# One decoder layer on one core: low-part products last in ten weight tiles, bank copies ahead of casts, eight block sums on another engine, one more pair by seven products

## The chip, the cores and the metric

The kernel runs on one core of one Trainium2 chip. A core has a matrix engine (TensorE, called PE in the profile; its weight loads are called PEld), a vector engine (VectorE, DVE), an engine for activation functions and copies (ScalarE, ACT), GpSimd (POOL) and a sync engine (SP) that only starts transfers. They run side by side and meet at semaphores. The metric is the device time of one execution in microseconds; the median of several runs is given. Operands lie in SBUF (128 partitions); matmul results are gathered in the banks of PSUM, which PE, DVE and ACT reach.

## The reference

One layer over x of 512 tokens by 1024 channels, all float32:

- u = RMSNorm(x); one input projection makes the gated-linear-unit halves, q, k, v, the output gate r, a rank-16 decay and two merge gates.
- Branch A: GLU, a causal depthwise convolution of 31 taps, LayerNorm over channels, swish, a projection.
- Branch B: gated linear attention of 4 heads in chunks of 64 tokens; per head an RMS norm over its 256 value channels, times silu(r), a projection.
- Merge: sigmoid(gA) * yA + sigmoid(gB) * yB, then the projection w_o, and the residual is added.
- Channel mixer: RMSNorm, an up projection to 2 x 2816 channels, a causal convolution of 3 taps, silu(a) * b, the down projection, residual; then a last RMSNorm.

## The kernel before, in words

**Products in three parts.** To keep float32 accuracy with a faster number type, each operand is split in a high and a low part (`hi`, `lo`), and one product is three matmuls, low x high, high x low, high x high (`mm3`, L395 to L397). A column tile of weights is 128 partitions by 1024 (eight k blocks of 128), so `col_tile` issues 24 matmuls of 512 columns into one PSUM bank, k after k.

**How weights come.** The list `order` names every weight block in the order of use. `load` starts the transfer of a block into one of four `raw` buffers (SP queue). `split_weight` then makes the parts: ACT casts `raw` to `whi` (L323, L342), and DVE subtracts, `wlo` = raw - whi (L324, L351). For the tiles named in the set `ADDED` the low part is made without DVE: ACT writes -whi into `wlo` (L344), and a DMA issued by POOL adds the block from HBM onto it (L345, accumulate). Four `whi` and four `wlo` buffers turn round. `weight(name, j)` takes the next block and calls `prefetch`, which splits up to two blocks ahead.

**Seven products for eight.** Where a matrix product can be cut in 2 x 2 quarters, the kernel uses seven quarter products in place of eight (`seven` for w_o and w_down, `Inner` for w_r and w_v, `up_seven` for the column tiles i of the up projection that stand in `UP_SEVEN`). They need sums of quarters of the weights. In `seven` a run has steps a11, a12, s1, n2, s4, n3, a22, in two halves d; the operand of n2 is a block `kept` plus the block `raw` that lands for it (L277), once in each half of the four runs, eight sums in all. Blocks that are summed by transfer are added by POOL's DMAs (L270, L303). In `up_seven` DVE and POOL form the sums (L285), the partial results are copied between banks by ACT (L1566, L1569, L1572, L1576) and DVE (L1578, L1579), and between its steps `beside` issues pieces of the ordinary tile of the same pair (`by_parts`).

**The heads.** In the loop over heads, head h's queries and keys are projected while the scores, states and outputs of head h - 1 are formed. `outputs` squares each half on ACT with a running sum (L1142), DVE adds epsilon (L1144), POOL raises to -1/2 (L443), and DVE scales (L1150); `gated` turns the result with PE (L1156). `decays` runs a scan on DVE and three exponentials on ACT (L1067, L1068, L1072). The convolution's taps (DVE, L813) are handed out between weight blocks by `fill`.

**After w_o.** `o_at` is called behind the products of a step; it turns the normalised residual rows of token tile 0 (behind n3's first half tile) and of tile 1 (behind a22's first) into channel order, with PE transposes (L474), a DVE multiply by the gain (L483), an ACT cast (L485) and a DVE subtraction (L486). The up projection's first tiles read them.

**What sets the order.** The start of the kernel, and the last products, are ordered by hand (`manual_schedule`). Elsewhere a planner places each engine's instructions ahead of time, by its own estimates of when each can start; on the chip each engine then runs its list strictly in that order. `tc.issue_after(x)` puts the instructions of a block behind x on x's engine.

Of the kernel before, what the change touches and what calls it, by code (L numbers as in the profile page):

```python
# [10 lines left out]
F32 = mybir.dt.float32  # L11
# [6 lines left out]
P = 128  # L18
# [24 lines left out]
ET = mybir.EngineType  # L43
ADDED = {("w_glu", 2 * k) for k in (2, 3, 4, 6, 7)} | {("w_qk", m) for m in range(0, KT)}
ADDED |= {(name, m) for name in ("w_gb", "w_gla") for m in range(KT)}
UP_SEVEN = (6, 7, 10, 11, 14, 15, 18)
UP_BESIDE = (1, 3, 4, 5, 9, 20, 13, 16, 17)
ADDED |= {("w_up", j) for i in UP_BESIDE for j in (i, FT + i)}
SEVEN = {"w_o": KT // 2, "w_down": FT // 2, "w_r": KT // 2, "w_v": KT // 2}


# [27 lines left out]
def trunk_layer(ctx: ExitStack, tc: tile.TileContext, a: dict, out: bass.AP):  # L79
# [65 lines left out]
    gate_up = cp.tile([P, HEADS * DK], F32R, name="gate_up")  # L145
    ones = cp.tile([P, P], F32, name="ones")
    mhalf = cp.tile([P, NT], F32, name="mhalf")
    shares = cp.tile([P, P], F32, name="shares")
    run64 = cp.tile([P, T], BF16, name="run64")
    keep = cp.tile([P, P], U8, name="keep")  # L150
# [2 lines left out]
    def load_consts():  # L153
        tc.keep_in_program_order(nc.sync.dma_start(pp, a["pp"]))
        nc.gpsimd.memset(shares, -1.0 / D)
        nc.gpsimd.memset(run64, 1.0)
        nc.gpsimd.memset(run64[:, 0:T:64], 0.0)

        kf = tmp(P)
        nc.gpsimd.memset(kf, 1.0)  # L160
        nc.gpsimd.affine_select(
            kf, kf, pattern=[[1, P]], compare_op=ALU.is_ge, fill=0.0, base=0, channel_multiplier=-1
        )
        nc.gpsimd.tensor_copy(keep, kf)
        nc.gpsimd.memset(att, 0.0)
# [106 lines left out]
    def operand(name, raw, pairs, step, d):  # L272

        if step == "s4":
            return kept[name, pairs, d, "b22"]
        if step == "n2" and name not in INNER:
            nc.vector.tensor_tensor(kept[name, pairs, d], kept[name, pairs, d], raw, ALU.add)  # L277
        return raw if step in ("a12", "n3") else kept[name, pairs, d]

    def up_operand(raw, i, s):  # L280
# [24 lines left out]
    def split_weight(between=None):  # L305
        if len(ready) < len(order):
            while len(raws) <= len(ready):
                load()
            raw = raws[len(ready)]
            name, spec = order[len(ready)]  # L310
            if name in SEVEN or name == "w_up7":
                raw = operand(name, raw, *spec) if name in SEVEN else up_operand(raw, *spec)
                n = raw.shape[-1]
                if name == "w_up7" and spec[1] == "m":
                    both = wp.tile([P, D], F32R, tag="raw", name=nm("wm"), bufs=4)
                    nc.scalar.copy(both[:, :T], raw)
# [6 lines left out]
                nc.scalar.copy(hi, raw)  # L323
                pace[0] = nc.vector.tensor_tensor(lo, raw, hi.bitcast(F32), ALU.subtract)  # L324
                if name in SEVEN:
                    sum_on(name, *spec)
                skipped = name in INNER and raws[len(ready)] is None
                ready.append((hi, lo))
                if not skipped:
                    load()  # L330
                return
            hi = wp.tile([P, D], F32R, tag="whi", name=nm("whi"), bufs=4)
            if order[len(ready)][0] == "w_low":
                nc.scalar.copy(hi, raw)
                if order[len(ready)][1] == 0:
                    part_lo = lambda t: t.rearrange("p (k c) -> p k c", c=P)[:, :, :RANK]
                    nc.vector.tensor_tensor(part_lo(hi), part_lo(raw), part_lo(hi.bitcast(F32)), ALU.subtract)
                ready.append((hi, None))
                load()
                return  # L340
            lo = wp.tile([P, D], F32R, tag="wlo", name=nm("wlo"), bufs=4)
            nc.scalar.copy(hi, raw)  # L342
            if order[len(ready)] in ADDED:
                pace[0] = nc.scalar.activation(lo, raw, AF.Copy, scale=-1.0)  # L344
                nc.gpsimd.dma_start(lo, a[name][spec], accum_op=ALU.add)  # L345
                ready.append((hi, lo))
                load()
                return
# [42 lines left out]
    def mm3(acc, l, r, first, last, more=False):  # L391
# [4 lines left out]
        nc.tensor.matmul(acc, lh, rl, start=False, stop=False, **kw)  # L396
        nc.tensor.matmul(acc, lh, rh, start=False, stop=last, **kw)  # L397

    def col_tile(w, acts, acc=None, lo=0, hi=T):

        if acc is None:
            acc = mm_bank()
        for k in range(KT):
            s = slice(k * P, (k + 1) * P)
            ah, al = acts[k]
            mm3(acc[:, lo:hi], (w[0][:, s], w[1][:, s]), (ah[:, lo:hi], al[:, lo:hi]), k == 0, k == KT - 1)
        return acc

    def row_half(name, j0, n, acts, nk, done, tok_inner, middle=None):
# [641 lines left out]
    class Head:  # L1051
# [77 lines left out]
        def outputs(self):  # L1129
            self.o = tp.tile([P, NT, DV], F32, tag="x", name=nm("o"), bufs=3)  # L1130
            for g in range(2):
# [7 lines left out]
                        nc.tensor.matmul(half, flat(self.q, p, 0), self.s[p], start=False, stop=True)  # L1139
                for i in range(2):  # L1140
                    half = po[:, i * DV : (i + 1) * DV]
                    nc.scalar.activation(junk(DV), half, AF.Square, scale=1.0 / 16.0, accum_out=ss[:, i : i + 1])  # L1142
                v = small(2, "var2")
                nc.vector.tensor_scalar(v, ss, EPS, None, ALU.add)  # L1144
                r = rsqrt(v, 2)
                for i in range(2):
                    t = 2 * g + i
# [25 lines left out]
    def between(h, i):  # L1173
# [4 lines left out]
        else:  # L1178
            gate_b(6 + i)

    heads = [Head(h) for h in range(HEADS)]
    for h in range(HEADS + 1):
        old = heads[h - 1] if h else None
        new = heads[h] if h < HEADS else None
        if new:
            new.decays()
            if h == 0:
                for y in sr.values():
                    behind(lambda: nc.scalar.activation(y, y, AF.Silu))
# [167 lines left out]
    def o_at(step, i):  # L1357
        if (step, i) == ("n3", 0):
            u2.extend(new_acts())
            first = tp.tile([P, D], F32, tag="gain", name=nm("f2"), bufs=1)  # L1360
            to_channels(normed[0], u2, 0, lambda g: first[:, g * T : (g + 1) * T])
        if (step, i) == ("a22", 0):
            to_channels(normed[1], u2, 1, lambda g: btmp())

    seven("w_o", O_PAIRS, mixed, o_complete, o_at)
# [186 lines left out]
    def up_seven(i, beside, done):  # L1552
# [15 lines left out]
        ys = att.rearrange("p a c -> p (a c)")[:, :H]  # L1568
        nc.scalar.copy(ys, y)  # L1569
        step("n2", x, wx, 1, False, 1)  # L1570
        prefetch(1)
        nc.scalar.activation(n1[:, :H], x, AF.Copy, scale=-1.0)  # L1572
        step("a12", n0[:, :H], wb, 1, False, 2)
        prefetch(2)
        step("n3", x, wn, 0, False, 1)
# [10 lines left out]
    def by_parts(w):  # L1586

        acc = mm_bank()
        for k in range(KT):
            s = slice(k * P, (k + 1) * P)  # L1590
            mm3(acc, (w[0][:, s], w[1][:, s]), acts2[k], k == 0, k == KT - 1)
            yield acc

    for gi, pairs in enumerate(GROUPS):
        acts = []
# [123 lines left out]
```

## Time and profile before

| | |
|---|---|
| median of 3 runs | 831.07 us (829.67 to 834.61) |
| the profiled execution | 828.47 us |
| its span on the core | 826.8 us |
| granted TensorE clock | 0.998 |
| PE busy | 813.3 us, 4090 matmuls |
| DVE busy | 676.8 us, 991 instructions |
| ACT busy | 471.0 us, 669 instructions |
| POOL busy | 123.1 us, 144 instructions |
| read from HBM | 133.84 MB |

The span is the time from the first to the last instruction of the core; 1.7 us of the profiled execution lie around it. The busy time of PE counts overlapped matmuls once, so a PE that waits shows as a gap between starts: matmuls of 512 columns follow each other every 0.23 us, those of 256 columns every 0.12 us.

### The profile page before, as it was taken

What the parts mean: (1) busy time and instruction counts of PE and PEld (TensorE: products, weight loads), DVE (VectorE), ACT (ScalarE), POOL (GpSimd) and SP (SyncE); (2) the same over time, 40 slices, a digit from 0 to 9 for tenths busy, and PEclk for the clock granted to TensorE, in tenths of its full rate; (3) what the DMA queues carried; (4) which work ended last, traced back from release to release, by engine and by line L of the source; (5) the groups of instructions that cost most, each with busy time, mean ns of one, the idle gap of its engine ahead of it and who ended that gap; (6) DMA issues with size and microseconds to landing.
All of it is one profiled execution on the core that took longest, in us unless ns stands there. A gap on an engine that the chain in (4) does not pass through costs nothing.

```text
span 826.8 us, 11023 instructions
## 1 busy us (share of the span) xinstructions
PE 813.3 (98%) x4090; PEld 689.9 (83%) x4090; DVE 676.8 (82%) x991; ACT 471.0 (57%) x669; POOL 123.1 (15%) x144
## 2 busy tenths in 40 slices
PE   8999999999999999999999999999999999999996
PEld 7988878878888888888888898888788888988885
DVE  6898978999989889854689768789858888588896
ACT  7664546695443553359344659655446543667554
POOL 2021101311122121000001012111112111220111
PEclk9999999999999999999999999999999999999999
DMA  9999849558666578221447539356835647557562
GB/s 324 310 327 222 209 116 230 129 160 211 150 131 154 134 195 202 77 102 51 153 92 205 183 116 237 93 146 153 217 93 149 166 89 217 153 153 202 131 128 101
DMA packets 50213, 136.65 MB, mean 165 GB/s; under 512 B 4624, under 2 KB 17184, under 8 KB 50160
## 3 DMA queue, kind: packets, MB, share of 16 engines
q1 hardware_dynamic: 37456, 90.91, 31.2%
q0 software_dynamic: 12528, 44.83, 30.5%
q8 instruction: 32, 0.52, 0.3%
q10 hardware_dynamic: 176, 0.20, 0.1%
q14 instruction: 21, 0.17, 0.1%
HBM read 133.84 MB, written 6.29 MB: 169 GB/s over the span
## 4 chain that ended last, share of the span: by engine, by line
PE 78%; DVE 11%; DMA 4%; issue 3%; ACT 2%; POOL 1%; SPq 0%; POOLq 0%; ACTq 0%; DVEq 0%
PE mm L396 22%; PE mm L395 22%; PE mm L397 22%; DVE c L813 4%; PE ax L395 2%; DMA wlo<-in_w_glu_dram 2%; PE mm L663 2%; PE ax L396 2%; PE ax L397 2%; DVE wlo L324 1%; DMA kept<-rows 1%; DMA x<-in_x_dram 1%; PE ax L1137 1%; DVE tmp L1378 1%; PE ax L474 0%
## 5 line engine op out<-in xcount | busy, mean ns | idle before, releaser
L395 PE MATMUL mm<-uh,wlo 128*128 128x512 f32 (+1 forms) x636 | 237.5, 374 | 3.5 <-DMA wlo<-in_w_glu_dram 1.9
L396 PE MATMUL mm<-ul,whi 128*128 128x512 f32 (+1 forms) x636 | 234.9, 369 | 0.2 <-DVE ul L486 0.2
L397 PE MATMUL mm<-uh,whi 128*128 128x512 f32 (+1 forms) x636 | 234.5, 369 | 0.0
L813 DVE SCALAR_TENSOR_TENSOR c<-h,pp,c 128x507 f32<-128x507 f32 (+20 forms) x240 | 169.9, 733 | 2.8
L395 PEld LDWEIGHTS mm<-uh,wlo 128*128 128x128 f32 x636 | 119.9, 189 | 22.9 <-DMA wlo<-in_w_glu_dram 2.1
L397 PEld LDWEIGHTS mm<-uh,whi 128*128 128x128 f32 x636 | 119.8, 188 | 20.5
L396 PEld LDWEIGHTS mm<-ul,whi 128*128 128x128 f32 x636 | 120.1, 189 | 18.7 <-DVE ul L486 0.7
L342 ACT CAST whi<-raw 128x1024 fp32r<-128x1024 f32 x94 | 97.4, 1042 | 36.7 <-PE mm L397 29.0
L344 ACT ACTIVATE wlo<-raw 128x1024 fp32r<-128x1024 f32 x47 | 49.5, 1058 | 69.6 <-PE mm L395 65.5
L323 ACT CAST whi<-raw 128x1024 fp32r<-128x1024 f32 (+1 forms) x53 | 54.0, 1027 | 52.6 <-PE mm L397 36.1
L324 DVE TENSOR_TENSOR wlo<-raw,whi 128x1024 fp32r<-128x1024 f32 (+1 forms) x53 | 65.8, 1249 | 11.5 <-ACT whi L323 11.0
L1378 DVE SCALAR_TENSOR_TENSOR tmp<-mm,pp,tmp 128x511 f32<-128x511 f32 (+1 forms) x88 | 64.5, 742 | 12.6 <-ACT tmp L1376 12.2
L351 DVE TENSOR_TENSOR wlo<-raw,whi 128x1024 fp32r<-128x1024 f32 x47 | 56.9, 1220 | 16.7 <-ACT whi L342 16.3
L323 ACT CAST whi<-kept 128x1024 fp32r<-128x1024 f32 (+1 forms) x44 | 44.3, 1009 | 37.7 <-PE mm L397 25.6
L324 DVE TENSOR_TENSOR wlo<-kept,whi 128x1024 fp32r<-128x1024 f32 (+1 forms) x44 | 52.3, 1196 | 4.3 <-ACT whi L323 4.1
L1376 ACT ACTIVATE tmp<-mm,pp 128x512 f32<-128x512 f32 x44 | 33.3, 775 | 11.6 <-PE mm L397 11.6
L1298 DVE TENSOR_TENSOR hres<-hres,mm 128x512 f32<-128x512 f32 (+1 forms) x49 | 32.4, 670 | 2.5 <-PE mm L397 2.3
L345 POOL DMA_DIRECT2D wlo<-in_w_up_dram x18 | 15.6, 866 | 95.5 <-ACT wlo L344 77.6
L396 PE MATMUL mm<-wlo,sh 128*128 128x512 f32 x66 | 25.9, 393 | 0.0
L397 PE MATMUL mm<-whi,sh 128*128 128x512 f32 x66 | 25.7, 390 | 0.0
L395 PE MATMUL mm<-h,wlo 128*128 128x512 f32 x64 | 25.4, 397 | 0.0
L395 PE MATMUL mm<-whi,sl 128*128 128x512 f32 x66 | 25.2, 391 | 0.2 <-ACT whi L323 0.2
(361 smaller groups left out, 1635.1 us busy)
## 6 DMA issues: line engine op xcount, KB each, us to landing
raw<-in_w_up_dram SPq DMA_DIRECT2D x44, 512.0 KB, 4.4
wlo<-in_w_up_dram POOLq DMA_DIRECT2D x18, 512.0 KB, 7.4
raw<-in_w_glu_dram SPq DMA_DIRECT2D x16, 512.0 KB, 5.9
raw<-in_w_down_dram SPq DMA_DIRECT2D x15, 512.0 KB, 5.1
kept<-in_w_down_dram POOLq DMA_DIRECT2D x10, 512.0 KB, 5.3
raw<-in_w_v_dram SPq DMA_DIRECT2D x8, 512.0 KB, 6.0
rows<-in_w_r_dram SPq DMA_DIRECT2D x16, 256.0 KB, 6.4
raw<-in_w_qk_dram SPq DMA_DIRECT2D x8, 512.0 KB, 5.1
```

What stands on the lines that cost most here:

```text
L323: nc.scalar.copy(hi, raw)
L324: pace[0] = nc.vector.tensor_tensor(lo, raw, hi.bitcast(F32), ALU.subtract)
L342: nc.scalar.copy(hi, raw)
L344: pace[0] = nc.scalar.activation(lo, raw, AF.Copy, scale=-1.0)
L351: pace[0] = nc.vector.tensor_tensor(lo, raw, hi.bitcast(F32), ALU.subtract)
L395: nc.tensor.matmul(acc, ll, rh, start=first, stop=False, **kw)
L396: nc.tensor.matmul(acc, lh, rl, start=False, stop=False, **kw)
L397: nc.tensor.matmul(acc, lh, rh, start=False, stop=last, **kw)
L813: nc.vector.scalar_tensor_tensor(y[:, s:], c[:, : T - s], w, y[:, s:], ALU.mult, ALU.add)
L1298: nc.vector.tensor_tensor(hres[t, n][:, c], hres[t, n][:, c], x[:, c], op)
L1376: nc.scalar.activation(z, acc, AF.Identity, bias=pp[:, PP_FB + m : PP_FB + m + 1], scale=w[2])
L1378: nc.vector.scalar_tensor_tensor(z[:, s:], acc[:, : T - s], w[j], z[:, s:], ALU.mult, ALU.add)
```

## The change

- **Low parts last.** A set `LOW_LAST_IN` names two tiles of w_glu (4 and 8) and the eight of w_qk. For them `col_tile` issues the sixteen products with the high weight part first, and the eight with the low weight part behind them. `by_parts` and `col_tile` share the new generator `col_products`; for all other tiles the order stays.
- **Bank copy ahead of the cast.** In `up_seven` the `prefetch(1)` behind step n2 moves behind the copy of L1572, and its ACT instructions are placed behind that copy.
- **Heads.** The addition of epsilon moves from DVE to POOL (with a new constant tile `eps` of two columns), and `decays` of heads 2 and 3 places its ACT instructions behind the last squares emitted so far.
- **w_o's end.** Token tile 1 is turned behind n3's second half tile, where it was behind a22's first.
- **Sums of n2.** The eight sums of L277 move from DVE to POOL.
- **Seven products for pair 19.** Up tile 19 and its partner are computed by `up_seven`, where they were two ordinary column tiles. It is the last pair ahead of the last run of w_down; its partner in the loop, tile 17, becomes the `beside` work.

```diff
-UP_SEVEN = (6, 7, 10, 11, 14, 15, 18)
+UP_SEVEN = (6, 7, 10, 11, 14, 15, 18, 19)
+LOW_LAST_IN = {("w_glu", 4), ("w_glu", 8)} | {("w_qk", m) for m in range(KT)}
...
     mhalf = cp.tile([P, NT], F32, name="mhalf")
+    eps = cp.tile([P, 2], F32, name="eps")
...
+        nc.gpsimd.memset(eps, EPS)
...
         if step == "n2" and name not in INNER:
-            nc.vector.tensor_tensor(kept[name, pairs, d], kept[name, pairs, d], raw, ALU.add)
+            nc.gpsimd.tensor_tensor(kept[name, pairs, d], kept[name, pairs, d], raw, ALU.add)
...
-                ready.append((hi, lo))
+                ready.append((hi, lo, (name, spec) in LOW_LAST_IN))
...
+    def col_products(w, acts, acc, lo=0, hi=T):
+
+        late = [(1, 0, k) for k in range(KT)] if w[2:] and w[2] else []
+        todo = [p for k in range(KT) for p in ([(0, 0, k), (0, 1, k)] if late else [(1, 0, k), (0, 1, k), (0, 0, k)])]
+        todo += late
+        for n, (low_w, low_a, k) in enumerate(todo):
+            l, r = w[low_w][:, k * P : (k + 1) * P], acts[k][low_a][:, lo:hi]
+            nc.tensor.matmul(acc[:, lo:hi], l, r, start=n == 0, stop=n == len(todo) - 1)
+            yield n
+
     def col_tile(w, acts, acc=None, lo=0, hi=T):
...
-            mm3(acc[:, lo:hi], (w[0][:, s], w[1][:, s]), (ah[:, lo:hi], al[:, lo:hi]), k == 0, k == KT - 1)
+        for _ in col_products(w, acts, acc, lo, hi):
+            pass
         return acc
...
-                    nc.scalar.activation(junk(DV), half, AF.Square, scale=1.0 / 16.0, accum_out=ss[:, i : i + 1])
+                    squared[0] = nc.scalar.activation(junk(DV), half, AF.Square, scale=1.0 / 16.0, accum_out=ss[:, i : i + 1])
                 v = small(2, "var2")
-                nc.vector.tensor_scalar(v, ss, EPS, None, ALU.add)
+                nc.gpsimd.tensor_tensor(v, ss, eps, ALU.add)
...
+        if squared[0] is None:
+            new.decays()
+        elif new:
+            with tc.issue_after(squared[0].ins):
+                new.decays()
         if new:
-            new.decays()
...
-        if (step, i) == ("a22", 0):
+        if (step, i) == ("n3", 1):
             to_channels(normed[1], u2, 1, lambda g: btmp())
...
         step("n2", x, wx, 1, False, 1)
-        prefetch(1)
-        nc.scalar.activation(n1[:, :H], x, AF.Copy, scale=-1.0)
+        copied = nc.scalar.activation(n1[:, :H], x, AF.Copy, scale=-1.0)
+        with tc.issue_after(copied.ins):
+            prefetch(1)
```

More of the change, by code (lines that the diff above doesn't have):

```diff
@@ L402, in col_tile @@
             acc = mm_bank()
-        for k in range(KT):
-            s = slice(k * P, (k + 1) * P)
-            ah, al = acts[k]
-            mm3(acc[:, lo:hi], (w[0][:, s], w[1][:, s]), (ah[:, lo:hi], al[:, lo:hi]), k == 0, k == KT - 1)
+        for _ in col_products(w, acts, acc, lo, hi):
+            pass
         return acc
@@ L1179, in between @@
             gate_b(6 + i)
+    squared = [None]
     heads = [Head(h) for h in range(HEADS)]
@@ L1588, in by_parts @@
         acc = mm_bank()
[L1589 to L1592, printed above, removed]
+        for n in col_products(w, acts2, acc):
+            if n % 3 == 2:
+                yield acc
     for gi, pairs in enumerate(GROUPS):
```

## The prediction

> **What bounds the kernel now.** I read the page's first part, the chain, then who PE waited for, then PE's timeline at each such wait.
>
> ```profile
> span 826.8 us, 11023 instructions
> PE 813.3 (98%) x4090; PEld 689.9 (83%) x4090; DVE 676.8 (82%) x991; ACT 471.0 (57%) x669; POOL 123.1 (15%) x144
> ...
> PE 78%; DVE 11%; DMA 4%; issue 3%; ACT 2%; POOL 1%; SPq 0%; POOLq 0%; ACTq 0%; DVEq 0%
> ```
>
> PE is the bound, and its matmuls are almost back to back; the change can win only what PE waits, or matmuls that it no longer runs. The waits of PE, longest first:
>
> ```profile
> PE mm L395 <- DMA wlo<-in_w_glu_dram: 1.9, 2, 1.7
> PE mm L395 <- DMA wlo<-in_w_qk_dram: 1.6, 1, 1.6
> ...
> PE ax L395 <- ACT mm L1572: 0.5, 1, 0.5
> ```
>
> These count from the modelled end of a matmul; the time lost is the gap between starts, less the ordinary 0.23 us (0.12 us for 256 columns). So each wait is priced from PE's timeline below.
>
> **The change part by part.**
>
> *Low parts last.* The first matmul that waits, in time order, is the first of a column tile, with `wlo` still in flight from POOL's accumulating transfer:
>
> ```profile
> 60.32 0.39 PE L397 MATMUL mm<-uh,whi 128*128 128x512 f32 x1
> 60.90 0.47 PE L395 MATMUL mm<-uh,wlo 128*128 128x512 f32 x1 [0.19 <-DMA wlo<-in_w_glu_dram]
> ...
> 104.31 0.39 PE L397 MATMUL mm<-whi,f 128*128 128x512 f32 x1
> 106.38 0.50 PE L395 MATMUL mm<-uh,wlo 128*128 128x512 f32 x1 [1.69 <-DMA wlo<-in_w_glu_dram]
> 106.72 0.39 PE L396 MATMUL mm<-ul,whi 128*128 128x512 f32 x1
> ...
> 181.58 0.39 PE L397 MATMUL mm<-uh,whi 128*128 128x512 f32 x1
> 183.56 0.50 PE L395 MATMUL mm<-uh,wlo 128*128 128x512 f32 x1 [1.60 <-DMA wlo<-in_w_qk_dram]
> ```
>
> Lost: 0.58 - 0.23 = 0.35; 2.07 - 0.23 = 1.84, and 0.11 in the slow restart (106.72 - 106.38 = 0.34); 1.98 - 0.23 = 1.75, and the like restart 0.11. Together 4.16 us. The number of matmuls stays. The low part is now needed sixteen matmuls later, 16 x 0.23 = 3.7 us, more than the longest lateness of 1.84, so I take all 4.16. `whi` comes free eight matmuls earlier, `wlo` as before; ACT casts can only start sooner.
>
> *Heads.* At the first head PE's eight transposes of `o` take longer than at the second head (chain in order of time):
>
> ```profile
> 212.11 0.38 PE L1156 MATMUL ax<-ident,o 128*128 128x128 f32 x2
> 212.66 1.15 PE L1156 MATMUL ax<-ident,o 128*128 128x128 f32 x6 [0.17 <-DVE o L1150]
> 213.57 0.47 PE L395 MATMUL mm<-uh,wlo 128*128 128x512 f32 x1
> ```
> ```profile
> 242.25 0.87 PE ax L1156 x8
> ```
>
> 1.46 - 0.87 = 0.59 us. What delays `o`, on ACT and DVE:
>
> ```profile
> 207.29 0.63 ACT L1067 ACTIVATE tmp<-b 128x512 f32<-128x512 f32 x1 [0.50 <-DVE h L832]
> ```
> ```profile
> 208.44 0.16 DVE L1144 TENSOR_SCALAR var<-ss 128x2 f32<-128x2 f32 x1
> ```
> ```profile
> L1447 POOL TENSOR_TENSOR var<-ss,var x4: 188/190/662, 808.1 to 821.4; 128x1 f32<-128x1 f32 x4
> ```
>
> The squares stood behind the next head's exponential (0.50 us idle and its own 0.63); `issue_after` puts it behind them. The epsilon add leaves DVE, where it queued among taps, for POOL: 0.19 to 0.66 us by the nearest POOL row, in front of POOL's power, with no hop between engines. POOL's queue also holds weight DMAs; the add stands at the place where the power already stood. `decays` has the whole query tile (24 x 0.23 = 5.4 us) as cover for about 1 us later exponentials. I take 0.6 us.
>
> *Channel order at w_o's end.* PE waits for DVE's `ul`:
>
> ```profile
> 474.86 0.28 PE L395 MATMUL mm<-uh,wlo 128*128 128x256 f32 x1
> 475.30 0.39 PE L396 MATMUL mm<-ul,whi 128*128 128x256 f32 x1 [0.16 <-DVE ul L486]
> ```
> ```profile
> 466.43 1.34 ACT L491 ACTIVATE un<-hres,rstd 128x512 f32<-128x512 f32 x2 [1.44 <-POOL rstd L443]
> ```
>
> Lost 0.44 - 0.12 = 0.32 us. The transposes now come twelve matmuls, 12 x 0.23 = 2.7 us, sooner; the products behind which they stand end at about 468.5, and their input `un` is ready at 466.43 + 1.34 = 467.8. Gain 0.3; if `un` came over 0.7 us later, PE would wait there, in front of products that are ready.
>
> *Bank copies.* Behind n2 PE needs ACT's copy L1572:
>
> ```profile
> 557.71 0.39 PE L397 MATMUL mm<-uh,whi 128*128 128x512 f32 x1
> 558.55 0.38 PE L395 MATMUL ax<-n3h,wlo 128*128 128x256 f32 x1 [0.45 <-ACT mm L1572]
> ```
> ```profile
> 555.52 1.05 ACT L323 CAST whi<-kept 128x1024 fp32r<-128x1024 f32 x1
> 557.39 0.83 ACT L1391 CAST sh<-v 128x768 fp32r<-128x768 f32 x1 [0.82 <-DVE v L1411]
> ```
>
> Lost 0.84 - 0.23 = 0.61, at the one place where it shows. The change puts the cast of 555.52 behind the copy, but not the cast `sh`, which waits for DVE and stood in front as well: if the planner leaves `sh` ahead, nothing is won at 558. Between 0 and 0.6 I take 0.4, for the copies of the other pairs may gain a little too. The cast that moves back has its `weight` call several products later as cover.
>
> *Sums of n2 on POOL.* Eight sums:
>
> ```profile
> L277 DVE TENSOR_TENSOR kept<-kept,raw x8: 679/1215/1219, 444.2 to 794.8; 128x1024 f32<-128x1024 f32 x7, 128x512 f32<-128x512 f32 x1
> ```
> ```profile
> L285 POOL TENSOR_TENSOR raw<-raw x7: 1287/1288/1799, 522.0 to 739.9; 128x512 f32<-128x512 f32 x7
> ```
>
> DVE is relieved of 1.22 us each. On POOL 1024 columns cost 2 x 1.29 = 2.6 us, at most 2 x 1.80 = 3.6. The sum sits at the end of a chain (sum, cast, subtraction, PE), and it cost PE time in the first run of w_down, where DVE is full:
>
> ```profile
> 584.34 0.62 PE L395 MATMUL mm<-whi,sl 128*128 128x512 f32 x2
> 585.12 0.72 PE L395 MATMUL mm<-whi,sl 128*128 128x512 f32 x2 [0.16 <-ACT whi L323]
> ```
> ```profile
> 565.00:587.00 22.00, 21.84 (x96) 17.39 (x95) 21.82 (x30) 11.72 (x14) 3.42 (x4) 1.00 0.73 160
> ```
>
> 0.78 - 0.46 = 0.32 us there. POOL (3.42 of 22 us busy) can start a sum as soon as the block's last reader is through, where DVE came to it late. But POOL's adds hold DVE up:
>
> ```profile
> 697.03 1.29 POOL L285 TENSOR_TENSOR raw<-raw 128x512 f32<-128x512 f32 x1 [14.03 <-DVE raw L285]
> ```
> ```profile
> 697.41 1.99 DVE L324 TENSOR_TENSOR wlo<-raw,whi 128x1024 fp32r<-128x1024 f32 x1
> ```
>
> The subtraction ends 1.08 us after POOL's add, near one ordinary 1.22: it stood still while POOL ran, 0.77 us. The Trainium skill, page SBUF — State Buffer, section "SBUF: two separate sides", calls this an exclusive lock on a shared port pair, held for a whole instruction, against DVE operations with two SBUF inputs; the trace agrees at 697.41. So a sum on POOL can take up to 2.6 us from DVE where it saved 1.22. DVE's reads of PSUM banks go on, and PE has some us of weights ahead, so I take +0.3 gained against 0.5 lost. In POOL's queue the block transfers L270 and L303 fall at most 2.6 us later; they serve steps after n2 and s4.
>
> *Pair 19.* Starts of the pairs in the last group (18 by seven products, then 19 by plain tiles, then w_down):
>
> ```profile
> 738.79 0.40 PE L395 MATMUL mm<-uh,wlo 128*128 128x512 f32 x1
> ...
> 759.99 0.40 PE L395 MATMUL mm<-uh,wlo 128*128 128x512 f32 x1
> ...
> 781.78 0.39 PE L395 MATMUL mm<-whi,yl 128*128 128x512 f32 x1
> ```
>
> A pair by seven takes 21.20, the plain one 21.79: 0.59 us gained, no more, because short matmuls cost more per column. DVE gets one more subtraction of 1024 columns (1.22), three operations of 512 (0.7 each) and two bank combinations (at most 0.7 each), some 4.7 us, and POOL two adds:
>
> ```profile
> 760.00:781.80 21.80, 21.80 (x99) 18.04 (x98) 18.99 (x28) 11.28 (x16) 1.73 (x2) 1.00 0.67 171
> ```
>
> DVE has 2.8 us free there, so about 2 us spill into w_down, whose steps a11 to s1 (10.9 us) are some cover. The first run of w_down also follows a pair by seven and lost the 0.32 above: I charge 0.4.
>
> **The sum.** 4.16 + 0.6 + 0.3 + 0.4 + 0.3 + 0.59 = 6.35 gained; 0.4 (w_down) + 0.5 (DVE held) lost: -5.45 us net. The profiled execution, 828.47 us (span 826.8 and 1.67 around it), becomes 823.0. The median of the runs shown is 2.60 above that execution, so I predict 831.07 - 5.45 = 825.6 us. A change of 0.5% (4.16 us, to 826.9 or 835.2) is about what a measurement of this kernel can tell.
>
> **The rivals.**
>
> *Given back at the heads (0.18).* Ahead of the heads DVE is full:
>
> ```profile
> 170.00:180.00 10.00, 10.00 (x46) 8.27 (x45) 10.00 (x18) 9.97 (x15) 1.73 (x2) 1.00 0.39 111
> ```
>
> PE would reach 212 some 4.2 us sooner, but if `o` comes no sooner, because DVE's list with its taps stays as it is, the 1.86 of w_qk and the 0.6 of the heads return as a longer wait before L1156, and perhaps 1.3 of w_glu: 825.6 + 3.8 = 829.4. For it: no free DVE time. Against: DVE's work up to there is paced by PE too, and the path squares to `o` gets about 2 us shorter.
>
> *Slower landings (0.10).* `eps` stands between two constant tiles, so every buffer laid out behind it moves by a few bytes, the weight buffers too. If transfers land slower for it, the place is the start, where the queues are full:
>
> ```profile
> 63.00:84.00 21.00, 21.00 (x94) 17.37 (x94) 18.89 (x26) 8.62 (x12) 3.50 (x4) 1.00 1.00 225
> ```
>
> Each 1% is 0.84 us by 84 us; the cover of 3.7 us for `wlo` hides about 2 to 4%. At 5% two to three us come back: 828. The page DMA: Bandwidth & Descriptors of the Trainium skill, section "How a descriptor splits into AXI transactions", has a start that isn't 256 B aligned cost an extra transaction; for a row of 4096 B that is 17 for 16, an estimate of 6%. No run here shows it.
>
> *Slower than before: the sums on POOL (0.12).* Where each of the eight holds DVE for all of its 2.6 us, DVE loses 1.4 net per sum, and where the cast behind it is late PE waits for the sum too. It decides from (5.45 + 4.16) / 8 = 1.2 us of PE wait per sum. At 1.4: 825.6 + 8 x 1.4 = 836.8. For it: 565 to 587 is 99% full. Against: none of PE's waits stands at 697, where DVE was held.
>
> *Bank copies do nothing.* Then 0.4 less, 826.0; it is inside the forecast.
>
> **How the numbers follow.** Forecast (gain of 3.5 to 7 us, 824 to 827.6): 0.60, most of it beyond 0.5%. Given back: 0.18, and slow landings 0.10, within 0.5% but for a few hundredths. Slower: 0.12. So faster 0.58, same 0.29, slower 0.13. The range: from all gained and nothing lost, 831.07 - 6.35 = 824.7, less the 1.4 by which the lowest run shown is under the median, 823; to the gain given back, 829.4, and the 3.5 by which the highest run is over it, 833. It leaves out the slower case. The forecast's own range is 824.0 to 827.6.
>
> **What would show it.** No PE wait on `wlo` at w_glu or w_qk; the first eight transposes in about 0.9 us; DVE `ul` no releaser of PE at w_o's end; L277 on POOL at 2.4 to 3.6 us, and DVE subtractions beside it of 1.8 us or more; a last pair of 21.2 us. Wrong if PE waits anew at n2 of w_down (casts behind POOL), at L1156, or at the start of the last w_down by more than 1 us, or if PE waits for `wlo` at w_glu although it is needed sixteen matmuls later.

## The result, and the profile after

The changed kernel takes 842.65 us (median; the kernel before took 831.2 beside it): ratio 1.0125, 95% interval 1.0099 to 1.0151. It is slower by some 10 us, where 5.5 us less was forecast. One of its four executions took 1367.69 us at a granted clock of 0.557; the ratio is taken without it, and the median of the other three is 842.06 us. The profiled execution took 842.06 us. Its page begins so (span; busy time of each engine, share, count; shares of the chain that ended last):

```profile
span 840.2 us, 11138 instructions
PE 820.4 (98%) x4126; PEld 693.9 (83%) x4126; DVE 680.3 (81%) x981; ACT 473.3 (56%) x675; POOL 149.6 (18%) x163
...
PE 68%; DVE 12%; DMA 9%; issue 4%; ACT 3%; POOL 1%; SPq 1%; POOLq 0%; ACTq 0%; DVEq 0%
```

PE's busy time grew by 7 us although more matmuls are short, and the chain runs over transfers for 9% instead of 4%. Who PE waited for, longest first (total us, times, longest):

```profile
PE mm L398 <- DVE yl L1407: 4.8, 2, 2.6
PE mm L409 <- DMA wlo<-in_w_up_dram: 2.3, 4, 1.2
PE ax L398 <- DVE wlo L327: 1.8, 2, 1.1
...
PE mm L398 <- DVE sl L1407: 1.1, 1, 1.1
PE mm L399 <- DVE wlo L327: 0.8, 1, 0.8
```

The waits for `wlo` of w_qk and the long ones at w_glu are gone, as forecast. The new ones all lie in the up and down projections. Starts of four places in the two timelines (us):

| | before | after |
|---|---|---|
| first transpose of the first head | 212.11 | 210.68 |
| first product of the first w_down | 565.01 | 563.80 |
| first product of the last w_down | 781.78 | 791.34 |
| last matmul | 819.89 | 833.34 |

Up to the first w_down the new kernel is 1.2 us ahead; from there to the last matmul it takes 269.5 us instead of 254.9.

The longest wait, in the timeline of all engines (rows that matter):

```profile
567.72 2.77 POOL L280 TENSOR_TENSOR kept<-kept,raw 128x1024 f32<-128x1024 f32 x1 [5.74 <-DVE wlo L327]
...
568.81 1.96 DVE L1414 TENSOR_TENSOR w<-w 128x256 f32<-128x256 f32 x1
...
570.80 0.62 ACT L1406 CAST yh<-w 128x512 fp32r<-128x512 f32 x1 [2.15 <-DVE w L1414]
...
572.00 0.68 DVE L1407 TENSOR_TENSOR yl<-w,yh 128x512 fp32r<-128x512 f32 x1
...
572.74 0.50 PE L398 MATMUL mm<-whi,yl 128*128 128x512 f32 x1 [2.63 <-DVE yl L1407]
```

DVE's operation of 256 columns at 568.81 starts while POOL's sum runs and ends 0.3 us behind it; the shortest of the eleven such in this trace takes 0.41 us. It is a subtraction too, but not of weights: it takes the difference of two halves of the activation `w`. From `w` come `yh` and then `yl`, which PE needs next.

### The profile page after: what moved, and what is told of

Its sections match the earlier page's. It is cut to its first block, busy times and chain, and to the rows that moved or that the text cites. A ratio compares the mean times of both kernels' runs of the same rounds, so it can differ in the third digit from the quotient of the medians.

```text
span 840.2 us, 11138 instructions
## 1 busy us (share of the span) xinstructions
PE 820.4 (98%) x4126; PEld 693.9 (83%) x4126; DVE 680.3 (81%) x981; ACT 473.3 (56%) x675; POOL 149.6 (18%) x163
## 4 chain that ended last, share of the span: by engine, by line
PE 68%; DVE 12%; DMA 9%; issue 4%; ACT 3%; POOL 1%; SPq 1%; POOLq 0%; ACTq 0%; DVEq 0%
PE mm L409 43%; PE mm L398 5%; PE mm L399 5%; PE mm L400 5%; DMA raw<-in_w_up_dram 3%; DVE wlo L327 3%; DVE tmp L1393 2%; DMA kept<-in_w_down_dram 1%; DMA wlo<-in_w_glu_dram 1%; DVE hres L1313 1%; DMA wlo<-in_w_up_dram 1%; PE ax L398 1%; PE ax L400 1%; PE ax L399 1%; SPq L106 1%
## 5 line engine op out<-in xcount | busy, mean ns | idle before, releaser
L409 PE MATMUL mm<-ul,whi 128*128 128x512 f32 (+1 forms) x592 | 220.7, 373 | 0.0
L409 PE MATMUL mm<-uh,whi 128*128 128x512 f32 (+1 forms) x592 | 220.3, 373 | 0.0
L409 PE MATMUL mm<-uh,wlo 128*128 128x512 f32 (+1 forms) x592 | 211.5, 378 | 2.6 <-DMA wlo<-in_w_up_dram 2.3
L409 PEld LDWEIGHTS mm<-uh,wlo 128*128 128x128 f32 x592 | 111.6, 189 | 21.6 <-DMA wlo<-in_w_up_dram 3.3
L409 PEld LDWEIGHTS mm<-uh,whi 128*128 128x128 f32 x592 | 111.5, 188 | 19.8
L409 PEld LDWEIGHTS mm<-ul,whi 128*128 128x128 f32 x592 | 111.8, 189 | 17.0
L326 ACT CAST whi<-raw 128x1024 fp32r<-128x1024 f32 (+1 forms) x56 | 57.3, 1026 | 61.1 <-PE mm L400 25.1
L327 DVE TENSOR_TENSOR wlo<-raw,whi 128x1024 fp32r<-128x1024 f32 (+1 forms) x56 | 68.6, 1231 | 12.2 <-ACT whi L326 11.7
L409 PE MATMUL mm<-h,whi 128*128 128x512 f32 x128 | 39.4, 389 | 0.0
L409 PEld LDWEIGHTS mm<-h,whi 128*128 128x128 f32 x128 | 24.0, 188 | 5.2 <-issue 0.2
```

The lines of the kernel that those rows point to most:

```text
L409: nc.tensor.matmul(acc[:, lo:hi], l, r, start=n == 0, stop=n == len(todo) - 1)
```

## The experiments

Each kernel below is told by its edit. The ratios are to the kernel before, run beside it on the same chip. The 95% intervals are about 0.2 to 0.3% to each side, 1.5 to 2.5 us, so the traces carry the smaller differences.

**The sums back on VectorE.**

```diff
-            nc.gpsimd.tensor_tensor(kept[name, pairs, d], kept[name, pairs, d], raw, ALU.add)
+            nc.vector.tensor_tensor(kept[name, pairs, d], kept[name, pairs, d], raw, ALU.add)
```

> The change with one thing undone: the eight n2 sums are on VectorE again. Theory SUMS (a sum on GpSimd holds VectorE and the transfers behind it in GpSimd's queue, and PE then waits in the FFN): PE's lost time between 540 and 830 us falls from about 15 us to 3-5 us; time 842.6 - 11 = about 831.5 us (829 to 834). Theory PAIR 19 (VectorE's list is overfull with one more pair by seven products): the waits of 2.8 us at 570 and 1.3 us at 654 stay, only some go; time 840 or more. Theory ORDER (the planner's other order, copies before casts, makes the FFN's waits): 841 to 843 us.

Measured: 834.8 us, ratio 1.0025 (1.0007 to 1.0044). The sums cost 1.0% of 832, 8.3 us. This one edit takes back most of the loss, so SUMS holds against its rivals, but not the 11 us that it named; what is left is slower than the kernel before by 0.25% and has other causes.

**eps in bytes that were unused.** The tile for -0.5 has 16 bytes and takes 32; `eps` goes into the rest.

```diff
-    mhalf = cp.tile([P, NT], F32, name="mhalf")
-    eps = cp.tile([P, 2], F32, name="eps")
+    mhalf_eps = cp.tile([P, NT + 2], F32, name="mhalf")
+    mhalf, eps = mhalf_eps[:, :NT], mhalf_eps[:, NT:]
```

> The change with its tile eps put into unused bytes behind the tile of -0.5, so that every buffer lies at the byte where it lay in the kernel before; no instruction moves. Theory SHIFT: PE's pitch for 512 columns goes back from 229 to 233 ns to 226.7 ns in w_r, w_v and w_conv (80 to 160 and 380 to 440 us), worth some 2.3 us, and the first weight's matmul comes at 5.9 us instead of 7.2; time 842.6 - 3.6 = 839 us (838 to 840). Rival (the pitch comes from the new order of the products or from other traffic): pitch and time stay, 842 to 843 us. The FFN's waits stay under both.

Measured: 839.49 us, ratio 1.0078 (1.0049 to 1.0107). PE's timeline at the same place of w_conv, first of the changed kernel, then of this one; twelve matmuls, first and last:

```profile
399.74 0.40 PE L409 MATMUL mm<-ch,wlo 128*128 128x512 f32 x1
...
402.30 0.40 PE L409 MATMUL mm<-ch,whi 128*128 128x512 f32 x1
```
```profile
399.64 0.39 PE L409 MATMUL mm<-ch,wlo 128*128 128x512 f32 x1
...
402.13 0.39 PE L409 MATMUL mm<-ch,whi 128*128 128x512 f32 x1
```

2.56 us for eleven starts, 0.2327 each, against 2.49 us, 0.2264. The pitch is back in w_r, w_v and w_conv, with the same instructions in the same order on every engine: SHIFT is right there. The other half of its claim is not: the first weight's matmul moved from 7.22 only to 7.07 us, not to 5.9. In the kernel before it stood at 6.89, so there was no 1.3 us to win back.

**Both.**

> Both of the above together: n2 sums on VectorE, eps in unused bytes. SUMS and SHIFT together and additive: 842.6 - 11 - 3.6 = 828 us (826 to 830), so faster than the kernel before by some 3 us. If PAIR 19 or ORDER are to blame for the FFN: 837 to 840 us.

Measured: 832.72 us, ratio 1.0003 (0.9981 to 1.0025). Between the two answers: the two edits win 10.2 us together, and 8.3 + 3.9 one by one, which is the same within the intervals. But the kernel is level with the one before, not 3 us under it. In its trace PE still takes 261.6 us from the first w_down to the last matmul, 6.7 more than before.

**The sums alone, on the kernel before.**

```diff
-            nc.vector.tensor_tensor(kept[name, pairs, d], kept[name, pairs, d], raw, ALU.add)
+            nc.gpsimd.tensor_tensor(kept[name, pairs, d], kept[name, pairs, d], raw, ALU.add)
```

> The kernel before with the n2 sums on GpSimd and nothing else. Theory SUMS alone: it loses by itself, 831 + 8 to 11 = 839 to 842 us, with a PE wait of 2 us or more for VectorE in the first pairs of the first w_down. If the sums cost only in company with pair 19 or with the other order of copies: 831 to 834 us.

Measured: 840.21 us, ratio 1.0089 (1.0059 to 1.0119), 7.4 us. The sums need no company to cost this. The wait that the expectation named comes as 1.3 us at the first w_down; the longest for DVE, 2.0 us for `sl`, stands at 690 us.

**Pair 19 by plain tiles again** (with the two edits above).

```diff
-UP_SEVEN = (6, 7, 10, 11, 14, 15, 18, 19)
+UP_SEVEN = (6, 7, 10, 11, 14, 15, 18)
```

> The change with n2 sums on VectorE, eps in unused bytes, and pair 19 again by plain tiles (three parts undone; low parts last, heads, channel order and bank copies stay). With pair 19 by seven products the last group and the first run of the last w_down were 5.1 us longer than in the kernel before, of which the waits of 0.8 us each at 738 and 760 stand ahead of pair 19. Theory PAIR 19 (its work fills VectorE and PE waits through the last w_down): 832.7 - 3.4 = 829.3 us, and the stretch from the last w_down's first product to its second run is 27.2 us instead of 30.0. If the charge of 0.4 against a gain of 0.59 was right: 832.9 us.

Measured: 832.55 us, ratio 1.0003 (0.9986 to 1.002): nothing won, so PAIR 19 fell as a statement on the time. The last w_down did get 2.8 us shorter, as it said (40.95 us to the last matmul, now 38.12). But other waits came, at the plain tiles, whose low part comes by POOL's transfer (waits of PE from 500 us on):

```profile
PE mm L409 <- DMA wlo<-in_w_up_dram: 4.3, 5, 2.6
PE mm L398 <- DVE yl L1407: 1.4, 1, 1.4
PE ax L398 <- DVE wlo L327: 0.9, 1, 0.9
```

**The casts ahead of the copy again** (pair 19 by seven products, the first two edits kept).

```diff
-        copied = nc.scalar.activation(n1[:, :H], x, AF.Copy, scale=-1.0)
-        with tc.issue_after(copied.ins):
-            prefetch(1)
+        prefetch(1)
+        nc.scalar.activation(n1[:, :H], x, AF.Copy, scale=-1.0)
```

> As the kernel with n2 sums on VectorE and eps in unused bytes (832.7 us), with the weight casts again ahead of the copy of x in a pair by seven products. Theory COPIES (a cast put behind the copy makes wlo late for the next step or the next tile): the waits on wlo at 547, 550, 644, 738 and 760 us, 4 us together, go, and the wait of 0.7 us on the copied bank at about 558 comes back: 832.7 - 3.3 = 829.4 us. If the copies are worth the 0.4 us of the forecast: 833.1 us.

Measured: 827.19 us, ratio 0.9939 (0.9916 to 0.9961). COPIES holds, and the price is more than expected: 0.64% of 832, 5.3 us beside pair 19 by seven products. PE's waits for `wlo` of w_up are gone, and the wait for the copied bank is back, 1.4 us in this execution.

**Low parts, heads and channel order alone** (all four costly parts undone).

> Of the change only: low parts last, the heads' two edits, the channel order at w_o's end, with eps in unused bytes. By the traces these three win 3.2 (w_glu and w_qk, a wait of 0.9 us left), 0.8 (heads) and 0 to 0.3 us: 4 to 4.5 us under the kernel before, ratio about 0.995. If PAIR 19 and COPIES each cost about 3.4 us and add up, it is 832.7 - 6.8 = 826 us. If the two share one cause and do not add up: 829 us. If the gain at w_glu and w_qk is given back later: ratio 1.000.

Measured: 825.23 us, ratio 0.9918 (0.9894 to 0.9942), 6.8 us under the kernel before. Neither sum of the expectation is quite met: with the casts ahead, pair 19 costs 827.19 - 825.23 = 2.0 us, which the intervals alone do not tell from nothing, and with the copies ahead it costs nothing. The copies cost 5.3 us beside pair 19 by seven products and 7.1 us (1.0003 - 0.9918) beside the plain pair; the two parts share waits. Why the transfers are late with the copies ahead shows beside pair 18. First the kernel with copies ahead and pair 19 plain (POOL, then PE):

```profile
755.37 0.88 POOL L348 DMA_DIRECT2D wlo<-in_w_up_dram  x1 [10.55 <-PE ax L400]
```
```profile
759.83 0.28 PE L400 MATMUL mm<-uh,wm 128*128 128x256 f32 x1
760.86 0.50 PE L409 MATMUL mm<-uh,wlo 128*128 128x512 f32 x1 [0.75 <-DMA wlo<-in_w_up_dram]
```

On ACT, ahead of that transfer, stand the copy, the cast that was put behind it, and -whi, which had to let another cast pass:

```profile
751.31 0.36 ACT L1586 ACTIVATE mm<-ax 128x256 f32<-128x256 f32 x1
751.61 1.03 ACT L345 CAST whi<-raw 128x1024 fp32r<-128x1024 f32 x1
...
753.91 1.05 ACT L347 ACTIVATE wlo<-raw 128x1024 fp32r<-128x1024 f32 x1
```

And the kernel with the casts ahead, at the same places on POOL and PE:

```profile
747.87 0.88 POOL L348 DMA_DIRECT2D wlo<-in_w_up_dram  x1 [7.95 <-ACT wlo L347]
```
```profile
756.32 0.28 PE L400 MATMUL mm<-uh,wm 128*128 128x256 f32 x1
756.43 0.40 PE L409 MATMUL mm<-uh,wlo 128*128 128x512 f32 x1
```

The transfer's row names PE's L400 as its releaser in the kernel with copies ahead, but its issue follows the end of -whi by 0.4 us in both kernels, so it is -whi that it waited for. The pair's last short matmul starts 4.5 us behind the transfer's issue in the one and 8.5 us behind it in the other. Such a transfer lands 7.8 and 7.4 us after its issue (medians of the 18 for w_up in the two); that of pair 18 with the copies ahead had landed when PE went on, 5.5 us after its issue. What `prefetch(1)` moves is not one cast: it is the cast, ACT's -whi behind it, and the transfer that waits for both.

What pair 19 does shows in the windows of the first run of the last w_down, with pair 19 by seven products and by plain tiles (columns PE, PEld, DVE, ACT, POOL busy, then clock, DMA share, GB/s):

```profile
779.30:801.00 21.70, 20.48 (x89) 16.04 (x88) 21.64 (x33) 11.65 (x17) 2.58 (x3) 1.00 0.79 185
```
```profile
778.20:800.00 21.80, 21.80 (x98) 18.03 (x97) 20.45 (x29) 11.39 (x15) 3.48 (x4) 1.00 0.62 132
```

DVE is full (21.64 of 21.70 us) for the whole run, and the last block sum, which is due there, comes late: it starts at 797.35 us, and the cast, which waited 2.43 us for it, at 798.65. With pair 19 by seven products, DVE and then PE:

```profile
797.35 1.21 DVE L280 TENSOR_TENSOR kept<-kept,raw 128x1024 f32<-128x1024 f32 x1
```
```profile
798.35 0.40 PE L400 MATMUL mm<-whi,sh 128*128 128x512 f32 x1
799.75 0.73 PE L398 MATMUL mm<-whi,sl 128*128 128x512 f32 x2 [1.00 <-ACT whi L326]
800.70 0.72 PE L398 MATMUL mm<-whi,sl 128*128 128x512 f32 x2 [0.22 <-ACT whi L326]
```

**Pair 19 alone, on the kernel before.**

```diff
-UP_SEVEN = (6, 7, 10, 11, 14, 15, 18)
+UP_SEVEN = (6, 7, 10, 11, 14, 15, 18, 19)
```

> The kernel before with pair 19 by seven products and nothing else. PAIR 19 by itself: 2.5 to 3.5 us slower than the kernel before, with waits of PE for VectorE in the pair and of about 1.5 us in the last w_down's first run. The forecast's terms (0.59 gained, 0.4 lost): 0.2 us faster.

Measured: 832.84 us, ratio 1.001 (0.9991 to 1.0028): 0.8 us slower (-0.7 to 2.3), which is less than PAIR 19 names and can't be told from the forecast's 0.2 us faster. The traces tell more. Two stretches, with pair 19 by plain tiles and by seven products (us):

| kernel | first product of the first w_down to that of the last | from there to the last matmul |
|---|---|---|
| before, plain | 216.77 | 38.11 |
| before, by seven | 216.45 | 40.20 |
| casts ahead (825 us), plain | 217.00 | 38.12 |
| casts ahead (827 us), by seven | 216.12 | 40.18 |

The pair wins 0.3 to 0.9 us and costs 2.1 us in the last w_down, both times: 1.2 to 1.8 us net. The cost has a place: 1.40 us between two starts in the last w_down's first run, 1.2 us lost, as PAIR 19 says.

This trace also shows something earlier, where nothing was changed:

```profile
PE mm L395 <- DMA wlo<-in_w_glu_dram: 4.0, 1, 4.0
PE mm L395 <- DMA wlo<-in_w_qk_dram: 1.3, 1, 1.3
```

The execution on which the forecast rests had 1.9 and 1.6 for the same instructions.

**The sums on GpSimd alone, on the kernel of 825 us.**

> The kernel with low parts last, heads and channel order alone (825.2 us), with the n2 sums on GpSimd. If the sums' loss adds to whatever is beside it (7.6 us on the kernel before, 7.8 under the whole change): 825.2 + 7.7 = 833 us. If it needs a full VectorE as pair 19 makes it: 828 us or less.

Measured: 831.43 us, ratio 0.9987 (0.9971 to 1.0004): 5.7 us over the kernel without them by the ratios, 6.2 by the medians. That is under the 7.4 and 8.3 us found above, but within the intervals; pair 19 and its full DVE aren't needed. PE's waits from 500 us on:

```profile
PE mm L398 <- DVE sl L1407: 2.0, 1, 2.0
PE mm L398 <- DVE yl L1407: 1.2, 1, 1.2
PE mm L399 <- DVE wlo L327: 1.2, 2, 0.7
```

Activations first (`sl`, `yl`), weights second. Ahead of the wait for `sl`, POOL's sum and the operation that makes `sl`:

```profile
677.06 2.12 POOL L280 TENSOR_TENSOR kept<-kept,raw 128x512 f32<-128x512 f32 x1 [3.49 <-DVE wlo L327]
...
677.99 2.01 DVE L1407 TENSOR_TENSOR sl<-v,sh 128x768 fp32r<-128x768 f32 x1
```

In the kernel before, the same operation takes 0.95 us; here it ends 0.8 us behind POOL's sum.

**Adds whose result nobody reads** (on the kernel of 825 us). The sum stays on VectorE; POOL adds columns of it into a tile that is otherwise a pad.

```diff
             nc.vector.tensor_tensor(kept[name, pairs, d], kept[name, pairs, d], raw, ALU.add)
+            b = kept[name, pairs, d]
+            for c in range(0, raw.shape[-1], T):
+                nc.gpsimd.tensor_tensor(spare_out[:, :504], b[:, c : c + 504], b[:, c + 8 : c + T], ALU.add)
```

> The same kernel with the sums on VectorE as they are, and behind each sum two more adds of 504 columns on GpSimd whose result nobody reads. They read the sum, and they stand in front of the transfers in GpSimd's queue. Theory HELD (GpSimd's add stops VectorE's subtractions and casts, whoever needs the result): VectorE operations of 1.8 us or more beside the adds, and 825.2 + 5 to 8 = 830 to 833 us. Theory CHAIN (the sum itself ends later, and the cast, the subtraction and PE behind it): 825.2 + 0 to 1.5 us, though VectorE is held. If the transfers behind the adds are what is late: PE waits for wlo or for casts of kept and raw blocks, without stretched VectorE operations ahead of them.

Measured: 836.57 us, ratio 1.0048 (1.003 to 1.0067): 10.8 us over the kernel without the adds by the ratios, 11.3 by the medians. CHAIN falls: nobody needs these results. HELD is seen (DVE, then POOL):

```profile
678.77 2.88 DVE L330 TENSOR_TENSOR wlo<-kept,whi 128x1024 fp32r<-128x1024 f32 x1
```
```profile
678.96 5.50 POOL L283 TENSOR_TENSOR pad<-kept 128x504 f32<-128x504 f32 x3
```

and who PE waited for:

```profile
PE mm L402 <- DVE wlo L330: 3.5, 3, 1.6
PE mm L401 <- DVE hres L1316: 3.1, 2, 2.3
PE ax L401 <- ACT mm L1584: 1.2, 1, 1.2
```

It is more than HELD's 8 us. DVE isn't relieved here, and the third possibility is there too: the longest gap between matmuls, from 693.73 us on, ends after a cast that had waited for a transfer of `kept`, issued behind the adds. On DVE's list `hres`, which PE waited for, stood behind that cast's subtraction.

```profile
694.35 0.62 ACT L329 CAST whi<-kept 128x512 fp32r<-128x512 f32 x1 [3.45 <-DMA kept<-in_w_down_dram]
...
696.43 0.47 PE L401 MATMUL mm<-whi,al 128*128 128x512 f32 x1 [2.31 <-DVE hres L1316]
```

How the loss divides between the two was not measured, and neither was it for the 8.3 us of the sums themselves.

**All buffers shifted alike** (on the kernel of 825 us). `eps` has its own tile again, and the pad at the other end of SBUF is 32 bytes shorter.

```diff
-PADS = (384, 2016, 768)
+PADS = (384, 1984, 768)
```

> The same kernel with eps in a tile of its own, and the pad at the other end of the memory 32 bytes shorter, so that the buffers laid out from that end (f and ch, operands of w_r, w_v and w_conv) move by 32 bytes too. Theory RELATIVE (PE loses where its two operands lie 32 bytes apart in a grid of 512): pitch 226.7 ns everywhere, time 825.2 us. Theory ABSOLUTE (an operand off the grid of 512 bytes costs by itself): pitch 230 ns or more in w_r, w_v and w_conv, or everywhere, 827.5 us or more.

Measured: 825.12 us, ratio 0.9905 (0.9883 to 0.9928), level with 825.23 us. RELATIVE holds, for a shift of 32 bytes; the grid of 512 bytes in the two theories was not tested. In w_conv PE again starts as many matmuls in 40 us as before (178), where the changed kernel starts 174; here the changed kernel, then this one (PE busy and count, clock, DMA share, GB/s):

```profile
388.00:428.00 40.00, 40.00 (x174) 1.00 0.37 107
```
```profile
388.00:428.00 40.00, 40.00 (x178) 1.00 0.43 119
```

**Copies ahead, and the low part last in w_up too** (pair 19 plain).

```diff
-LOW_LAST_IN = {("w_glu", 4), ("w_glu", 8)} | {("w_qk", m) for m in range(KT)}
+LOW_LAST_IN = {("w_up", j) for i in UP_BESIDE for j in (i, FT + i)} | {("w_glu", 4), ("w_glu", 8)} | {("w_qk", m) for m in range(KT)}
```

> The kernel with the bank copies ahead of the casts and pair 19 by plain tiles (832.5 us), and now the low part also last in the w_up tiles whose low part POOL's transfer completes. Theory LATE TRANSFER (the cast behind the copy starts the transfer of wlo about 3 us later, and PE waits for it in the tile behind each pair by seven products): the waits on wlo from w_up, 6 us together, fall under 1 us, 832.5 - 5 = 827.5 us. If the copies cost through VectorE or the banks: 831 us or more.

Measured: 829.69 us, ratio 0.9966 (0.9945 to 0.9986); 2.9 us won of the 5 expected, and of the 7.1 that the copies cost beside the plain pair. The waits for `wlo` of w_up, 4.3 us in the view above, are all gone, as LATE TRANSFER has it. What is left over 825.2 us lies in one place (PE from 500 us on):

```profile
PE mm L398 <- DVE yl L1407: 3.5, 1, 3.5
PE ax L398 <- DVE wlo L327: 0.8, 1, 0.8
```

The wait for `yl` at the start of the first w_down is in the traces of all kernels here with the copies ahead; of those with the casts ahead it is only where the sums are on GpSimd. Ahead of it DVE had stood idle behind a cast, and the cast had waited for a block of w_down to land (ACT, then DVE):

```profile
560.43 1.05 ACT L326 CAST whi<-kept 128x1024 fp32r<-128x1024 f32 x1 [4.81 <-DMA kept<-in_w_down_dram]
```
```profile
561.51 1.23 DVE L327 TENSOR_TENSOR wlo<-kept,whi 128x1024 fp32r<-128x1024 f32 x1 [4.17 <-ACT whi L326]
```

That the copies make this transfer late too is likely, but it wasn't tried by itself.

**Heads and channel order alone** (of the kernel of 825 us).

```diff
-LOW_LAST_IN = {("w_glu", 4), ("w_glu", 8)} | {("w_qk", m) for m in range(KT)}
+LOW_LAST_IN = set()
```

> Heads and channel order alone (as the kernel of 825.2 us, but with every column tile's products in the old order). The forecast priced low parts last at 4.16 us from one execution; in the traces of two other kernels with the old order PE lost 5.8 and 8.0 us on wlo at w_glu and w_qk. Theory LANDINGS VARY (the wait is longer in most executions than in the one profiled, and sixteen matmuls hide it): 825.2 + 5.5 to 6.5 = about 831 us, with a wide spread from run to run. If 4.16 was right: 829.4 us, and 3 us of the 7 come from elsewhere in the change.

Measured: 831.05 us, ratio 0.9989 (0.9967 to 1.0012). Low parts last are worth 0.71% of 832, 5.9 us: LANDINGS VARY. The heads' edits and the channel order are together worth 0.9 us, which can't be told from nothing.

**The low part last in all such tiles of w_glu** (on the kernel of 825 us).

```diff
-LOW_LAST_IN = {("w_glu", 4), ("w_glu", 8)} | {("w_qk", m) for m in range(KT)}
+LOW_LAST_IN = {x for x in ADDED if x[0] in ("w_glu", "w_qk")}
```

> The kernel of 825.2 us with the low part last in all tiles of w_glu that POOL's transfer completes, so also in the one at 71 us where 0.1 to 1.8 us were left in the traces. LANDINGS VARY: 825.2 - 0.5 = 824.7 us, no wait for wlo of w_glu. If another tile then waits in its place: 825.2 us or more.

Measured: 824.3 us, ratio 0.9905 (0.9876 to 0.9933). PE waits for no `wlo` between 60 and 200 us any more. The 0.9 us to the kernel without it is inside the uncertainty; it has the lowest median here, 0.95% under the kernel before and 2.2% under the change.

**The account.** Each row is the difference of two ratios above, times 832 us:

| part, undone in this order | us |
|---|---|
| block sums on GpSimd | +8.3 |
| 32-byte shift by eps | +1.8 |
| bank copies ahead of casts | +5.3 |
| pair 19 by seven products | +1.7 |
| low parts last | -5.9 |
| heads and channel order | -0.9 |
| sum | +10.3 |

The ratio of the change, 1.0125, is 10.4 us. The rows add up to it by construction, since each starts where the one above ends; that is no proof of them. Each is known to 2 to 3 us, and in another order they would differ. The first, the third and the fifth stand clear of that by themselves; the shift and pair 19 rest on their traces.

## Why the prediction was wrong

The forecast was 825.6 us, at the low side of a range to 833; 842.65 lies beyond it. The gains came, one larger than forecast. The costs were priced far too low or not at all. Step by step:

- **Low parts last: mechanism right, term too small.** 4.16 us forecast, 5.9 measured. The step "so I take all 4.16" took one execution's waits for the waits of the kernel. In the four traces with the old order PE waited 1.9, 5.1, 4.0 and 1.8 us in all for `wlo` of w_glu; in the last three the granted clock fell to between 0.50 and 0.65 for some 4.5 us behind the longest such wait; in the forecast's own execution it did not. The heads' first transposes start at 212.1, 218.2, 217.5 and 213.6 us there, and between 207.9 and 210.1 in the ten traces with low parts last and no shift between the buffers.
- **Heads and channel order: as forecast, too small to measure.** The eight transposes took

```profile
210.84 0.87 PE ax L1166 x8
```

  as forecast ("about 0.9 us"), and `ul` no longer releases PE. Of the 0.9 us forecast together, 0.9 was found, with an interval that holds zero. Nothing was given back at the heads: that rival fell.
- **Bank copies: a gain of 0.4 forecast, a loss of 5.3.** The step that failed: "The cast that moves back has its `weight` call several products later as cover." The cover was counted for one cast. Three instructions in a row moved, the last of them a transfer that lands 7.4 to 7.8 us after its issue (median; 5.5 at pair 18), and its cover there was 8.5 us with the casts ahead and 4.5 us with the copies ahead. The step listed the cast and not the POOL transfer behind it. Without the waits for these transfers 2.9 us came back; the rest goes with the wait for `yl` at the first w_down, whose cause was not tried by itself.
- **Sums on POOL: a loss of 0.2 net forecast, 8.3 measured.** The duration was right:

```profile
L280 POOL TENSOR_TENSOR kept<-kept,raw x8: 2506/2790/3309, 436.9 to 807.7; 128x1024 f32<-128x1024 f32 x7, 128x512 f32<-128x512 f32 x1
```

  (2.6 to 3.6 forecast), and so was the held DVE. The step that failed: "PE has some us of weights ahead, so I take +0.3 gained against 0.5 lost." What DVE was held from was not only weights: between pairs and w_down it makes the activations `yl` and `sl`, and of these PE has none ahead. The argument against the rival, that no wait of PE stands at 697, took a place where DVE was held with a weight's subtraction. The rival's 1.4 us of PE wait per sum is nearer to the 8.3 / 8 = 1.04 found than the forecast's net 0.2 / 8. The Trainium skill, page SBUF — State Buffer, section "SBUF: two separate sides", has a GpSimd instruction that starts first block a DVE operation with two SBUF inputs entirely until its end. The trace of the change agrees: 1.96 us for the operation of 0.41, with its end 0.3 us behind POOL's.
- **Pair 19: a gain of 0.19 net forecast, a loss of 1.2 to 1.8 beside casts that stand ahead, of 0 beside copies.** The gain of 0.59 was right in size (0.3 and 0.9 in two traces). The step that failed: "I charge 0.4." The charge was the wait that another pair by seven had left behind it, and 2.1 us came; "some cover" in w_down was not there, since DVE had no free time through the whole first run. The waits at 798 us in the kernel of 827 us are 1.0 and 0.2 us in the rows, and 1.8 us between starts.
- **The eps tile: seen, but on the wrong path, and with no term in the sum.** It cost 1.8 us beside sums on VectorE and 3.9 beside sums on POOL. "Slower landings" was the rival. The landings stayed: for the 44 loads of w_up, 4.8 us in the kernel of 825 us and 4.7 with all buffers shifted, and for the 16 of w_glu, near the start, 6.0 and 5.8, with the same number of packets. So the transactions by which the rival's estimate came to 6% cost nothing visible here. It was PE's pitch that rose.

The rival that ends slower had a chance of 0.12 and stood for one mechanism alone. Three terms of cost failed, each for its own reason, but two of them alike: an instruction was moved or slowed, and only its first follower was priced. A fourth cost, the shift, had no term.

## What to carry to other kernels

Where work is moved behind something, follow it to the last instruction that hangs on it, and set the cover against that transfer's landing time, not against the cast. An addition on GpSimd took time from VectorE as well in the traces shown; price it by the most urgent thing VectorE makes near it, which may be an activation that nobody has ahead. And a wait for a transfer, taken from one execution, is one draw: take it from several before pricing its removal.

## What the runs showed of the hardware

- **PE's pitch depends on how its two operands lie to each other.** With the buffers of one end of the memory moved by 32 bytes and those of the other not, a matmul of 512 columns in w_conv came every 0.2327 us instead of 0.2264. With both moved by the same 32 bytes it did not: 178 started in 40 us, as before. Which distances cost, and why, was not tried.
- **A wait of PE can cost more than its length.** Behind the wait of 2.63 us at 572.74 in the changed kernel the granted clock (column behind the count) was 0.62 for 4.5 us:

```profile
572.70:577.20 4.50, 4.46 (x13) 0.62 0.99 220
577.20:582.00 4.80, 4.80 (x23) 1.00 0.42 65
```

  Thirteen matmuls instead of some twenty: about 1.6 us on top of the wait. Behind the wait of 2.18 us that ended at 799.82 the clock stayed at 1.00. The sixteen traces together, from 20 us on, with the waits as the rows give them: all seven of 2.3 us or more were followed by such a stretch, at 0.50 to 0.65; of the nine of 1.6 to 2.2 us four were (1.78, 1.99, 2.07 and 2.15 us) and five were not (1.60, 1.67, 1.69, 1.99 and 2.18 us). The Trainium skill, page TensorE: Matmul & The Clock Gate, section "What's actually happening", has the clock halve after an idle window of about 3.4 us; here waits from 1.78 us on were enough in some executions.
- **The same transfers land unlike from one execution to the next.** With the old order of products PE waited 1.9, 5.1, 4.0 and 1.8 us for `wlo` of w_glu in four traces, with all else ahead of that place alike or nearly so.
